# A hybrid decoder step: a lighter state-space mixer, with the sample states read out by C's high and low parts

## The chip, the cores and the metric

The kernel runs on one core of one Trainium2 chip. The metric is the device time of one execution in microseconds. A profiled execution gives a trace with the instructions of each engine: PE is TensorE (PEld its weight loads), DVE is VectorE, ACT is ScalarE, POOL is GpSimd, SP is SyncE, which here only issues DMAs. L333 means line 333 of the kernel before.

## The reference

One step of a one-layer hybrid decoder over 512 prompt tokens and 64 sample tokens (8 sequences of 8), width 2048. A combined projection of the normed input feeds a state-space branch (Mamba-2) and a sliding-window attention branch. Both are projected back, gated, added and projected once more. The part that the change touches, for one head, cut to its core:

```
Acs = cumsum(dt * A)                             # falls along a chunk
L[l, s] = exp(Acs[l] - Acs[s]) for s <= l, else 0
y_diag[l] = sum_s (C[l] . B[s]) L[l, s] X[s]
y_off[l]  = (C[l] . state_before) * exp(Acs[l])
state     = state * exp(Acs[last]) + sum_s exp(Acs[last] - Acs[s]) B[s] X[s]
g = (y_diag + y_off + d_skip * xs) * silu(z)
y = g * rsqrt(mean(g * g over the 512 of a group) + eps) * w
```

There are 64 heads of 64 in 8 groups; each group has its own B and C of 128 states. The prompt has four chunks of 128 tokens; each sample sequence is a chunk of 8 with a state of its own that is read, used and updated. Everything is float32, and all updated states are outputs.

## The kernel before

Activations lie with features on the partitions and all 576 tokens along the row. A projection takes a float32 weight apart into a high part `wh` (rounded to fp32r, a float format that PE takes in one pass) and a low part `wl` (the rest), and so the activations (`ah`, `al`); each product is three fp32r matmuls (L333). `run_main` goes over tiles of 128 output columns, 16 steps of six matmuls each, and calls `pump` after each step. A weight chunk is 1024 by 128, loaded by SP (L68) and split by ACT (L75) and DVE (L76), one chunk ahead. A finished tile stands in one of two PSUM buffers until its `take` has copied it out (for the convolved tiles `take_conv`, L809 to L811).

Everything else is written as generators: `pump` advances the first of the `quick` ones and, at rate 9 of 8, the first of the `jobs`. `yield` and `wait(n)` set after how many steps of the main stream a part is put. A planner of the framework then orders each engine's queue by its own estimate of when inputs are ready, with the order of writing as priority; on the chip each engine takes its queue in order. PSUM has besides a pool of four banks (`bank`), and each stage has pools of SBUF tiles (`kten` draws from N_K, `cten` from N_C); an instruction that needs a tile waits until one is free.

The stages: norm and first projections, 24 pairs of projection tiles by a seven-product scheme (L437), attention, then the state-space stage with its eight groups, then the three closing projections. In the state-space stage each group has six convolved tiles (B, C and four of x) and some gate tiles in the main stream, and one `ssd_job`, which starts when the group's last x tile is out, so beside the next group's projections:

- `lmat` builds the L matrix of four heads at a time: it loads the decay sums of the four heads, the same row to every partition (L859), subtracts each head's own sum per partition and takes the minimum with 0 on DVE (L862), and takes the exponential on ACT (L864). `mmat` multiplies with C.B (L870).
- Per chunk: transposes (L897), the old state by C (L912), the new state (L916), the diagonal part (`pairs_mm`, L848).
- `ssd_sample` does the eight sequences in two halves of four, each half in two pairs. It loads two states (L995), transposes each on PE (L1045), copies the transposed state `sT` out of PSUM on ACT (L1047), computes the addition to the state (L1054) and updates it (L1060), and reads out: a float32 matmul of C's eight columns, padded to 32 (`cpad`), by `sT` (L1066), into 32 partitions of a bank `pyo`. After each half the bank is copied (`yo`, L1073), turned back by four transposes (L1077) and multiplied into `ea` (L1080).
- The group's gated norm: squares and their sum on POOL (L957, L959), taken apart into two fp32r parts (L963, L964), summed over partitions by a matmul with ones so that every partition has the sum (L969); root (L970), reciprocal (L971), product (L975) and store to `y_d` (L977).

After the last group the attention output is loaded (L1242) and split (L1250, L1251) for the first closing projection.

Of the kernel before, what the change touches and what calls it, by code (L numbers as in the profile page):

```python
# [20 lines left out]
NB = 8  # L21
NQ = 8
NS = NB * NQ
T = NP_TOK + NS
TH = T // 2
DI = 4096
H = 64
G = 8
# [21 lines left out]
MIXES_S = (1, 1, 1, 1, 1, 1, 1, 1)  # L50
N_E = 14
N_C = 18
N_K = 18


def AP(t, off, dims):
    return bass.AP(t.tensor, t.offset + off, [list(d) for d in dims])
# [23 lines left out]
def hybrid(ctx, tc, x_prompt, x_sample, cache_k, cache_v, state_conv, state_ssm, norm_w, w_in, conv_w,  # L81
# [5 lines left out]
    ten, vec, act, pool, sync = nc.tensor, nc.vector, nc.scalar, nc.gpsimd, nc.sync  # L87
# [30 lines left out]
    xb_d = scratch([D // 2, TH], "xb_d")  # L118
    oh_d = scratch([HEADS * BL], "oh_d")
    ea_d = scratch([H, T], "ea_d")  # L120
    acs_d = scratch([H, T], "acs_d")
    e4_d = scratch([H, 4], "e4_d")
    e8_d = scratch([H, 8], "e8_d")

    def pers_tile(shape, name):
        return pers.tile(shape, F32, tag=name, name=name)

    ident = pers_tile([P, P], "ident")
    tri = pers_tile([P, P], "tri")
# [6 lines left out]
    sinks_s = pers_tile([P, 4], "sinks_s")  # L136
    dt_n = pers_tile([P, 5, H], "dt_n")
    dtd_n = pers_tile([P, 5, H], "dtd_n")
    acs_n = pers_tile([P, 5, H], "acs_n")
    cd_b = pers_tile([P, H, 4], "cd_b")  # L140
    dec_s = pers_tile([P, 32, 8], "dec_s")
    ones = pers.tile([P, P], F32R, tag="ones", name="ones")
# [129 lines left out]
    def kten(shape, name="k", dt=F32):  # L272
        return now["k"].tile(shape, dt, tag=now["kt"], name=name)
# [27 lines left out]
    def wait(n):  # L301
        for _ in range(n):
            yield
# [441 lines left out]
    def dt_job(dtT, bt):  # L745
# [14 lines left out]
        vec.scalar_tensor_tensor(out=x_, in0=x_, scalar=0.0, in1=p_, op0=ALU.max, op1=ALU.add)  # L760
        yield

        vec.tensor_scalar(out=s, in0=x_, scalar1=bt[:, 1:2], scalar2=-1.0, op0=ALU.mult, op1=ALU.mult)
        vec.tensor_tensor_scan(out=s2, data0=rst, data1=s, initial=0.0, op0=ALU.mult, op1=ALU.add)
        sync.dma_start(out=acs_d, in_=s2)
        act.activation(p_, s2, AF.Exp)
        sync.dma_start(out=ea_d, in_=p_)
        e4 = now["s"].tile([H, 4], F32, tag="e4", name="e4", bufs=1)
        e8 = now["s"].tile([H, 8], F32, tag="e8", name="e8", bufs=1)
# [5 lines left out]
        for lo, hi, n in ((0, 512, P), (512, T, 8)):  # L775
            v = s2[:, lo:hi].rearrange("p (c l) -> p c l", l=n)
            o = s[:, lo:hi].rearrange("p (c l) -> p c l", l=n)
            vec.tensor_tensor(out=o, in0=v[:, :, n - 1:n].to_broadcast([H, (hi - lo) // n, n]), in1=v,
                              op=ALU.subtract)
        act.activation(s, s, AF.Exp)  # L780
        vec.tensor_tensor(out=s, in0=s, in1=x_, op=ALU.mult)
        yield from wait(14)
        for srcT, dst in ((x_, dt_n), (s, dtd_n), (s2, acs_n)):
            ps = bank()
            for b in range(4):
                ten.transpose(ps[:, b * H:(b + 1) * H], srcT[:, b * P:(b + 1) * P], ident[:H, :H])
            ten.transpose(ps[:NS, 4 * H:5 * H], srcT[:, 512:T], ident[:H, :H])
            vec.tensor_copy(dst[:, 0:4, :], ps[:, 0:4 * H].rearrange("p (b h) -> p b h", h=H))
            vec.tensor_copy(dst[:NS, 4, :], ps[:NS, 4 * H:5 * H])
            yield  # L790
# [60 lines left out]
    def head_rows(t_, ea, g, c0, n):  # L851
        for hf in range(2):
            sync.dma_start(out=t_[64 * hf:64 * hf + 64], in_=AP(ea, (8 * g + hf) * T + c0, [[0, 64], [2 * T, 4], [1, n]]))

    def lmat(g, c0, n, blk, rows):
        out = []
        for q in range(2):
            l_ = kten([P, 4, P], "L")
            sync.dma_start(out=l_[:rows, :, :n], in_=AP(acs_d, (8 * g + 4 * q) * T + c0, [[0, rows], [T, 4], [1, n]]))  # L859
            for i in range(4):  # L860
                h = 8 * g + 4 * q + i
                vec.tensor_scalar(out=l_[:rows, i, :n], in0=l_[:rows, i, :n], scalar1=acs_n[:rows, blk, h:h + 1],  # L862
                                  scalar2=0.0, op0=ALU.subtract, op1=ALU.min)
            act.activation(l_[:rows, :, :n], l_[:rows, :, :n], AF.Exp)  # L864
            out.append(l_)
        return out

# [5 lines left out]
    def ssd_job(g):  # L873
# [89 lines left out]
        act.activation(th, tot, AF.Copy)  # L963
        pool.tensor_tensor(out=tl, in0=tot, in1=th, op=ALU.subtract)  # L964
        yield from wait(8)
        for s in range(2):
            ps = bank()
            for i, t_ in enumerate((th, tl)):
                ten.matmul(ps[:, :TH], ones, t_[:, s * TH:(s + 1) * TH], start=i == 0, stop=i == 1)  # L969
            act.activation(sqr[:, s * TH:(s + 1) * TH], ps[:, :TH], AF.Sqrt, bias=eps, scale=1.0 / 512)  # L970
        vec.reciprocal(sqr, sqr)  # L971
        yield
        for t in range(4):
            j = 4 * g + t
            vec.scalar_tensor_tensor(out=xs[t], in0=xs[t], scalar=prm[:, 240 + j:241 + j], in1=sqr, op0=ALU.mult,  # L975
# [11 lines left out]
    def ssd_sample(g, xs, bT, cT):  # L987
# [19 lines left out]
        for q in range(2):  # L1007
# [3 lines left out]
            pool.tensor_tensor(out=t_, in0=bq.unsqueeze(1).to_broadcast([P, 4, P]),  # L1011
                               in1=own.unsqueeze(2).to_broadcast([P, 4, P]), op=ALU.mult)
            bb.append(t_)
        cpad = kten([P, NB, 32], "cpad")
        pool.memset(cpad, 0.0)
        pool.tensor_copy(cpad[:, :, 0:8], cs_.rearrange("p (b q) -> p b q", q=8))
        yield
        px = bank()
        for t in range(4):
# [12 lines left out]
        yield from wait(2)  # L1032
        ea = kten([P, 4, NS], "eas")
        head_rows(ea, ea_d, g, 512, NS)
        for hb in range(2):
            pyo = bank()
            for b2 in range(2):
                sts, sTs = nxt, []
                b0 = 4 * hb + 2 * b2
# [2 lines left out]
                for i in range(2):  # L1042
                    ps = bank([P, 4, P])
                    for t in range(4):
                        ten.transpose(ps[:, t, :], sts[i][:, t, :], ident)  # L1045
                    sT = kten([P, 512], "sT")
                    act.activation(sT, ps.rearrange("p t n -> p (t n)"), AF.Copy)  # L1047
                    sTs.append(sT)
                    yield
                for u in range(2):  # L1050
                    ps = bank([P, 2, 2, P])
# [10 lines left out]
                                                     op0=ALU.mult, op1=ALU.add)  # L1062
                    yield
                for i in range(2):
                    bl = 2 * b2 + i
                    ten.matmul(pyo[32 * bl:32 * bl + 32, :], cpad[:, 4 * hb + bl, :], sTs[i], start=True, stop=True,  # L1066
                               tile_position=(0, 32 * bl))
                yield
                for i in range(2):
                    b = 4 * hb + 2 * b2 + i  # L1070
                    sync.dma_start(out=oview[b, 512 * g:512 * g + 512].rearrange("(t p) n -> p t n", p=P), in_=sts[i])
            yo = kten([P, 512], "yo")
            act.activation(yo, pyo, AF.Copy)  # L1073
            yield from wait(2)
            ps = bank([P, 4, P])
            for t in range(4):
                ten.transpose(ps[:, t, :], yo[:, t * P:(t + 1) * P], ident)  # L1077
            for t in range(4):
                v = ea[:, t, 32 * hb:32 * hb + 32].rearrange("p (b q) -> p b q", q=8)
                vec.tensor_tensor(out=v, in0=ps[:, t, :].rearrange("p (b q) -> p b q", q=32)[:, :, 0:8], in1=v,  # L1080
                                  op=ALU.mult)
            yield
        pd = bank([P, 4, P])
        pairs_mm(pd, xd[:NS], ls, NS)
        vec.tensor_tensor(out=ea, in0=pd[:, :, :NS], in1=ea, op=ALU.add)
# [363 lines left out]
```

## Time and profile before

| | us |
|---|---|
| median of 3 runs | 3288.77 (3287.61 to 3290.53) |
| profiled execution, its time | 3288.66 |
| profiled execution, span of the trace | 3286.6 |
| PE busy | 3191.1 |
| PE weight loads busy | 3025.2 |
| DVE busy | 1791.6 |
| ACT busy | 1336.9 |
| POOL busy | 332.1 |

Matmuls are pipelined, so the duration of one in the trace includes its way through the array; what a matmul costs in a full queue is the time from its start to the next one's start. A float32 matmul leaves two records, an fp32r matmul or a transpose one. A row of the timeline has start, length, engine, line, operation, output and inputs, shape and how many are merged; behind it in brackets idle time and what ended it. A row of the groups has busy time, mean ns of one, and the idle time ahead of them with its releasers. A row of the waits has the total, the number and the longest.

### The profile page before, as it was taken

How to read it: one execution, taken by the hardware profiler on the slowest of the kernel's cores; microseconds unless marked ns; L12 is line 12 of the kernel's file. 1: busy time of each engine (PE TensorE's matmuls, PEld its weight loads, DVE VectorE, ACT ScalarE, POOL GpSimd, SP SyncE). 2: the span in 40 equal slices, each digit the busy share in tenths (PEclk: the TensorE clock that was granted, in tenths of full speed). 3: DMA queues.
4: the chain of work that ended last, by engine and by line, in shares of the span. 5: the costliest groups of instructions: out<-in, count | busy, mean ns of one | idle time of the engine just before them, and what ended most of it. 6: DMA issues, size and time to landing. Idle time of an engine off the chain costs nothing. (4 is left out here: it accounts for less than half of the span.)

```text
span 3286.6 us, 57410 instructions
## 1 busy us (share of the span) xinstructions
PE 3191.1 (97%) x23323; PEld 3025.2 (92%) x23323; DVE 1791.6 (55%) x3290; ACT 1336.9 (41%) x2335; POOL 332.1 (10%) x443
## 2 busy tenths in 40 slices
PE   7989999999999999999999999999979999999997
PEld 6989999999988988989899898888869999999997
DVE  7666666622644444376786776766742242423554
ACT  5434444422445546345454445444531121211443
POOL 3200000000010110112212121121110000000111
PEclk9999999999999999999999999999989999999999
DMA  6564444433333243354554544645573353533555
GB/s 201 146 152 121 120 130 116 118 104 91 94 110 94 88 122 105 94 144 129 142 151 130 155 123 126 167 111 139 153 237 105 107 163 106 149 105 96 156 163 162
DMA packets 696823, 429.17 MB, mean 131 GB/s; under 512 B 39600, under 2 KB 661952, under 8 KB 696368
## 3 DMA queue, kind: packets, MB, share of 16 engines
q1 hardware_dynamic: 668000, 397.50, 43.5%
q10 hardware_dynamic: 15552, 15.93, 1.5%
q0 software_dynamic: 13008, 12.09, 1.4%
q8 instruction: 183, 3.00, 0.4%
q14 instruction: 80, 0.66, 0.1%
HBM read 361.00 MB, written 74.67 MB: 133 GB/s over the span
## 5 line engine op out<-in xcount | busy, mean ns | idle before, releaser
L333 PE MATMUL ps<-ah,wh 128*128 128x288 f32 (+2 forms) x5408 | 1235.7, 300 | 29.0 <-ACT craw L811 16.5
L333 PE MATMUL ps<-ah,wl 128*128 128x288 f32 (+2 forms) x5408 | 1231.9, 300 | 2.0 <-DVE wl L76 1.7
L333 PE MATMUL ps<-al,wh 128*128 128x288 f32 (+2 forms) x5408 | 1232.3, 299 | 0.0
L75 ACT ACTIVATE wh<-raw 128x1024 fp32r<-128x1024 f32 x538 | 570.0, 1060 | 1305.0 <-PE ps L333 866.4
L76 DVE TENSOR_TENSOR wl<-raw,wh 128x1024 fp32r<-128x1024 f32 x538 | 670.0, 1246 | 705.0 <-ACT wh L75 697.2
L333 PEld LDWEIGHTS ps<-ah,wh 128*128 128x128 f32 x5408 | 896.8, 191 | 54.5 <-issue 21.3
L333 PEld LDWEIGHTS ps<-ah,wl 128*128 128x128 f32 x5408 | 897.7, 191 | 28.4 <-issue 22.7
L333 PEld LDWEIGHTS ps<-al,wh 128*128 128x128 f32 x5408 | 898.3, 191 | 17.0 <-issue 14.5
L437 PE MATMUL ps<-ah,wh 128*128 128x288 f32 x768 | 227.7, 296 | 5.8 <-DVE w L391 5.8
L437 PE MATMUL ps<-ah,wl 128*128 128x288 f32 x768 | 228.0, 297 | 2.0 <-DVE wl L76 2.0
L437 PE MATMUL ps<-al,wh 128*128 128x288 f32 x768 | 227.6, 296 | 0.0
L827 DVE SCALAR_TENSOR_TENSOR cacc<-craw,prm,cacc 128x600 f32<-128x600 f32 x144 | 126.9, 890 | 52.0 <-ACT cacc L825 50.8
L437 PEld LDWEIGHTS ps<-ah,wh 128*128 128x128 f32 x768 | 145.4, 189 | 6.0 <-issue 6.0
L437 PEld LDWEIGHTS ps<-ah,wl 128*128 128x128 f32 x768 | 145.3, 189 | 2.5 <-DVE wl L76 2.5
L437 PEld LDWEIGHTS ps<-al,wh 128*128 128x128 f32 x768 | 145.4, 189 | 0.1
L377 DVE TENSOR_TENSOR raw<-raw 128x1024 f32<-128x1024 f32 x96 | 117.0, 1221 | 42.4 <-DMA raw<-in_w_in_dram 41.5
L1368 POOL TENSOR_TENSOR res<-res,fw 128x128 f32<-128x128 f32 (+3 forms) x35 | 31.8, 933 | 819.8 <-ACT junk L1364 787.5
L1060 DVE SCALAR_TENSOR_TENSOR s<-s,dec_s,bank 128x128 f32<-128x128 f32 x256 | 70.6, 341 | 61.0 <-PE bank L1054 61.0
L1314 DVE TENSOR_TENSOR sg<-ps,sg 128x576 f32<-128x576 f32 x32 | 24.2, 757 | 126.1 <-PE ps L333 126.1
L593 DVE CUSTOM_DVE_ANT_0 sc<-bank,bm 128x256 f32<-128x256 f32 (+1 forms) x128 | 43.8, 388 | 79.9 <-PE bank L589 71.1
L862 DVE TENSOR_SCALAR L<-L,acs_n 128x128 f32<-128x128 f32 (+1 forms) x320 | 75.0, 302 | 18.4 <-DMA L<-acs_d 18.1
L864 ACT ACTIVATE L<-L 128x512 f32<-128x512 f32 (+1 forms) x80 | 46.2, 585 | 63.7 <-DVE L L862 53.6
(503 smaller groups left out, 3617.3 us busy)
## 6 DMA issues: line engine op xcount, KB each, us to landing
raw<-in_w_in_dram SPq DMA_DIRECT2D x306, 512.0 KB
raw<-in_w_ssm_branch_dram SPq DMA_DIRECT2D x64, 512.0 KB
raw<-in_w_out_dram SPq DMA_DIRECT2D x64, 512.0 KB
L<-acs_d SPq DMA_DIRECT2D x64, 256.0 KB
s<-in_state_ssm_dram SPq DMA_DIRECT2D x64, 256.0 KB
out_dram<-s SPq DMA_DIRECT2D x64, 256.0 KB
raw<-in_w_attn_branch_dram SPq DMA_DIRECT2D x32, 512.0 KB
zs<-z_d SPq DMA_DIRECT2D x32, 288.0 KB
```

Of the source, the lines that this page charges most:

```text
L75: pin(nc.scalar.activation(wh, raw, AF.Copy))
L76: pin(nc.vector.tensor_tensor(out=wl, in0=raw, in1=wh, op=ALU.subtract))
L333: ten.matmul(sums[i][:, s, :part.shape[1]], a[:, kk, :], part, start=(k == 0 and q == 0), stop=(k == last and q == 2))
L377: vec.tensor_tensor(out=s_[x], in0=s_[a], in1=s_[b], op=op)
L437: ten.matmul(st[p]["ps", i][:, :TH], a[:, k, :], b, start=i < 4 and k == 0 and q == 0, stop=k == 7 and q == 2, skip_group_check=i >= 4)
L593: vec.tensor_tensor_reduce(out=s_[:, i, lo:256], in0=ps[:, i, lo:256], in1=bm[j][:, i, lo:256], scale=1.0, scalar=-3e38, op0=ALU.add, op1= ...
L827: vec.scalar_tensor_tensor(out=acc[:, :600], in0=raw[:, i:i + 600], scalar=prm[:, i * 48 + j:i * 48 + j + 1], in1=acc[:, :600], op0=ALU.mu ...
L862: vec.tensor_scalar(out=l_[:rows, i, :n], in0=l_[:rows, i, :n], scalar1=acs_n[:rows, blk, h:h + 1], scalar2=0.0, op0=ALU.subtract, op1=ALU ...
L864: act.activation(l_[:rows, :, :n], l_[:rows, :, :n], AF.Exp)
L1060: vec.scalar_tensor_tensor(out=sts[i][:, t, :], in0=sts[i][:, t, :], scalar=dec_s[:, 4 * g + t, b:b + 1], in1=ps[:, v, i, :], op0=ALU.mult ...
L1314: vec.tensor_tensor(out=sq(sg), in0=ps[:, :, :TH], in1=sq(sg), op=ALU.mult)
L1368: pool.tensor_tensor(out=res[b][:, qs], in0=res[b][:, qs], in1=fw[:rows, qs], op=ALU.mult)
```

## The change

In `lmat` the decay sums are kept with the other sign (`nacs`). One DVE operation takes the maximum with the partition's own sum for four heads together, and ACT takes four exponentials with scale -1 and the own sum as bias.

In the norm, one row of the sum over partitions is copied out (not the root on all 128), sent to DRAM (`rms_d`) and read back as 64 by 9; root and reciprocal are taken there, and the result goes to DRAM and comes back on all partitions. The four DMAs are issued by ACT, with `wait(6)` twice in between.

In `ssd_sample`, C's high part and low part stand side by side in one stationary tile of 128 columns per sequence (`cw_`, zero but for the eight columns of the sequence in each 64). The transposed state is taken apart as well (`sTh` by ACT, `sTl` by DVE), and two fp32r matmuls per sequence add into one bank for all eight sequences. That bank is copied once, and four float32 matmuls with `two` (two unit matrices of 64, one under the other) turn it back and add both halves. `N_K` goes from 18 to 19.

```diff
-N_K = 18
+N_K = 19
+    rms_d = scratch([G, 2, T], "rms_d")
+    two = pers_tile([P, 64], "two")
+    for hf in range(2):
+        pl = slice(64 * hf, 64 * hf + 64)
+        vec.tensor_copy(two[pl], ident[pl, pl])
...
-        vec.tensor_scalar(out=s, in0=x_, scalar1=bt[:, 1:2], scalar2=-1.0, op0=ALU.mult, op1=ALU.mult)
+        vec.tensor_scalar(out=s, in0=x_, scalar1=bt[:, 1:2], scalar2=None, op0=ALU.mult)
-        act.activation(p_, s2, AF.Exp)
+        act.activation(p_, s2, AF.Exp, scale=-1.0)
...
+            h = 8 * g + 4 * q
+            vec.tensor_tensor(out=l_[:rows, :, :n], in0=l_[:rows, :, :n],
+                              in1=nacs_n[:rows, blk, h:h + 4].unsqueeze(2).to_broadcast([rows, 4, n]), op=ALU.max)
             for i in range(4):
-                h = 8 * g + 4 * q + i
-                vec.tensor_scalar(out=l_[:rows, i, :n], in0=l_[:rows, i, :n], scalar1=acs_n[:rows, blk, h:h + 1],
-                                  scalar2=0.0, op0=ALU.subtract, op1=ALU.min)
-            act.activation(l_[:rows, :, :n], l_[:rows, :, :n], AF.Exp)
+                act.activation(l_[:rows, i, :n], l_[:rows, i, :n], AF.Exp, scale=-1.0,
+                               bias=nacs_n[:rows, blk, h + i:h + i + 1])
...
-            act.activation(sqr[:, s * TH:(s + 1) * TH], ps[:, :TH], AF.Sqrt, bias=eps, scale=1.0 / 512)
-        vec.reciprocal(sqr, sqr)
-        yield
+            act.activation(sqr[0:1, s * TH:(s + 1) * TH], ps[0:1, :TH], AF.Copy)
+        act.dma_start(out=rms_d[g, 0:1, :], in_=sqr[0:1, :])
+        rt = now["s"].tile([NS, 9], F32, tag="rt", name="rt", bufs=1)
+        act.dma_start(out=rt, in_=rms_d[g, 0].rearrange("(a b) -> a b", b=9))
+        yield from wait(6)
+        act.activation(rt, rt, AF.Sqrt, bias=eps[:NS], scale=1.0 / 512)
+        vec.reciprocal(rt, rt)
+        act.dma_start(out=rms_d[g, 1].rearrange("(a b) -> a b", b=9), in_=rt)
+        act.dma_start(out=sqr, in_=AP(rms_d[g, 1], 0, [[0, P], [1, T]]))
+        yield from wait(6)
...
-        cpad = kten([P, NB, 32], "cpad")
-        pool.memset(cpad, 0.0)
-        pool.tensor_copy(cpad[:, :, 0:8], cs_.rearrange("p (b q) -> p b q", q=8))
+        cw_ = [kten([P, 4, P], "cw", F32R) for _ in range(2)]
+        for q in range(2):
+            act.activation(cw_[q], ident.unsqueeze(1).to_broadcast([P, 4, P]), AF.Identity, scale=0.0)
+            c4 = cs_[:, 32 * q:32 * q + 32].rearrange("p (b q) -> p b q", q=8)
+            hi, lo = (AP(cw_[q], c0 + 32 * q, [list(cw_[q].ap[0]), [P + 8, 4], [1, 8]]) for c0 in (0, 64))
+            act.activation(hi, c4, AF.Copy)
+            vec.tensor_tensor(out=lo, in0=c4, in1=hi, op=ALU.subtract)
...
+        pyo = bank()
         for hb in range(2):
-            pyo = bank()
...
-                    sT = kten([P, 512], "sT")
-                    act.activation(sT, ps.rearrange("p t n -> p (t n)"), AF.Copy)
-                    sTs.append(sT)
+                    sTh, sTl = (kten([P, 4, P], n_, F32R) for n_ in ("sTh", "sTl"))
+                    act.activation(sTh, ps, AF.Copy)
+                    vec.tensor_tensor(out=sTl, in0=ps, in1=sTh, op=ALU.subtract)
+                    sTs.append((sTh, sTl))
...
-                    bl = 2 * b2 + i
-                    ten.matmul(pyo[32 * bl:32 * bl + 32, :], cpad[:, 4 * hb + bl, :], sTs[i], start=True, stop=True,
-                               tile_position=(0, 32 * bl))
+                    for d in range(2):
+                        ten.matmul(pyo, cw_[hb][:, 2 * b2 + i, :], sTs[i][d].rearrange("p t n -> p (t n)"),
+                                   start=b0 + i + d == 0, stop=b0 + i + d == 8, skip_group_check=True)
...
-            yo = kten([P, 512], "yo")
-            act.activation(yo, pyo, AF.Copy)
-            yield from wait(2)
-            ps = bank([P, 4, P])
-            for t in range(4):
-                ten.transpose(ps[:, t, :], yo[:, t * P:(t + 1) * P], ident)
-            for t in range(4):
-                v = ea[:, t, 32 * hb:32 * hb + 32].rearrange("p (b q) -> p b q", q=8)
-                vec.tensor_tensor(out=v, in0=ps[:, t, :].rearrange("p (b q) -> p b q", q=32)[:, :, 0:8], in1=v,
-                                  op=ALU.mult)
-            yield
+        yo = kten([P, 512], "yo")
+        act.activation(yo, pyo, AF.Copy)
+        yield from wait(2)
+        ps = bank([P, 4, NS])
+        for t in range(4):
+            ten.matmul(ps[:, t, :], yo[:, t * P:(t + 1) * P], two, start=True, stop=True)
+        vec.tensor_tensor(out=ea, in0=ps, in1=ea, op=ALU.mult)
+        yield
```

More of the change, by code (lines that the diff above doesn't have):

```diff
@@ L120, in hybrid @@
     ea_d = scratch([H, T], "ea_d")
-    acs_d = scratch([H, T], "acs_d")
+    nacs_d = scratch([H, T], "nacs_d")
     e4_d = scratch([H, 4], "e4_d")
     e8_d = scratch([H, 8], "e8_d")
+    rms_d = scratch([G, 2, T], "rms_d")
     def pers_tile(shape, name):
@@ L138, in hybrid @@
     dtd_n = pers_tile([P, 5, H], "dtd_n")
-    acs_n = pers_tile([P, 5, H], "acs_n")
+    nacs_n = pers_tile([P, 5, H], "nacs_n")
     cd_b = pers_tile([P, H, 4], "cd_b")
@@ L761, in dt_job @@
         yield
-        vec.tensor_scalar(out=s, in0=x_, scalar1=bt[:, 1:2], scalar2=-1.0, op0=ALU.mult, op1=ALU.mult)
+        vec.tensor_scalar(out=s, in0=x_, scalar1=bt[:, 1:2], scalar2=None, op0=ALU.mult)
         vec.tensor_tensor_scan(out=s2, data0=rst, data1=s, initial=0.0, op0=ALU.mult, op1=ALU.add)
-        sync.dma_start(out=acs_d, in_=s2)
-        act.activation(p_, s2, AF.Exp)
+        sync.dma_start(out=nacs_d, in_=s2)
+        act.activation(p_, s2, AF.Exp, scale=-1.0)
         sync.dma_start(out=ea_d, in_=p_)
@@ L777, in dt_job @@
             o = s[:, lo:hi].rearrange("p (c l) -> p c l", l=n)
-            vec.tensor_tensor(out=o, in0=v[:, :, n - 1:n].to_broadcast([H, (hi - lo) // n, n]), in1=v,
+            vec.tensor_tensor(out=o, in0=v, in1=v[:, :, n - 1:n].to_broadcast([H, (hi - lo) // n, n]),
                               op=ALU.subtract)
@@ L782, in dt_job @@
         yield from wait(14)
-        for srcT, dst in ((x_, dt_n), (s, dtd_n), (s2, acs_n)):
+        for srcT, dst in ((x_, dt_n), (s, dtd_n), (s2, nacs_n)):
             ps = bank()
@@ L858, in lmat @@
             l_ = kten([P, 4, P], "L")
-            sync.dma_start(out=l_[:rows, :, :n], in_=AP(acs_d, (8 * g + 4 * q) * T + c0, [[0, rows], [T, 4], [1, n]]))
+            sync.dma_start(out=l_[:rows, :, :n], in_=AP(nacs_d, (8 * g + 4 * q) * T + c0, [[0, rows], [T, 4], [1, n]]))
+            h = 8 * g + 4 * q
+            vec.tensor_tensor(out=l_[:rows, :, :n], in0=l_[:rows, :, :n],
+                              in1=nacs_n[:rows, blk, h:h + 4].unsqueeze(2).to_broadcast([rows, 4, n]), op=ALU.max)
             for i in range(4):
-                h = 8 * g + 4 * q + i
-                vec.tensor_scalar(out=l_[:rows, i, :n], in0=l_[:rows, i, :n], scalar1=acs_n[:rows, blk, h:h + 1],
-                                  scalar2=0.0, op0=ALU.subtract, op1=ALU.min)
-            act.activation(l_[:rows, :, :n], l_[:rows, :, :n], AF.Exp)
+                act.activation(l_[:rows, i, :n], l_[:rows, i, :n], AF.Exp, scale=-1.0,
+                               bias=nacs_n[:rows, blk, h + i:h + i + 1])
             out.append(l_)
```

## The prediction

> **What bounds the kernel now.** I read the busy shares first, then the state-space stage (the eight groups, 1344 to 2411 us) as one window, then TensorE's waits.
>
> ```profile
> PE 3191.1 (97%) x23323; PEld 3025.2 (92%) x23323; DVE 1791.6 (55%) x3290; ACT 1336.9 (41%) x2335; POOL 332.1 (10%) x443
> ...
> 1344.00:2411.00 1067.00, 1043.42 (x7602) 942.16 (x7600) 734.78 (x1478) 504.09 (x879) 193.82 (x260) 0.99 0.51 137
> ...
> PE ps L333 <- ACT craw L811: 16.5, 6, 4.6
> PE bank L969 <- ACT th L963: 13.0, 1, 13.0
> PE bank L1066 <- ACT sT L1047: 1.1, 2, 0.7
> ```
>
> The second row is the window: its length, then busy time on PE, PE's weight loads, DVE, ACT and POOL, granted clock, DMA share. PE is busy 1043 of 1067 us there; DVE is at 69%, ACT at 47%, DMA at 51%. PE's queue is in order, and in nearly every gap that the state-space work leaves, the projection matmuls of L333 stand ready. So a PE microsecond taken out of the stage is a microsecond of the kernel, as long as no new wait takes its place. The waits for the old read-out (L1066) are 1.1 us in all: its inputs are not late today. The two waits that matter are at the evictions of projection tiles (L811) and once behind the norm of the last group (L969).
>
> **Part 1, the read-out: C times the state, L1066.** It goes from 64 full-float matmuls with 32 stationary columns (two records each) to 128 one-record fp32r matmuls with 128 columns. I take prices as start-to-start, since ends are modelled.
>
> ```profile
> 1852.67 0.29 PE L333 MATMUL ps<-ah,wh 128*128 128x288 f32 x1
> 1852.90 1.05 PE L1066 MATMUL bank<-sT,cpad 128*32 128x512 f32 x2
> 1853.88 0.40 PE L333 MATMUL ps<-ah,wh 128*128 128x288 f32 x1
> 1854.11 0.42 PE L333 MATMUL ps<-al,wh 128*128 128x288 f32 x2
> 1854.46 1.04 PE L1066 MATMUL bank<-sT,cpad 128*32 128x512 f32 x2
> 1855.44 0.66 PE L1045 MATMUL bank<-ident,s 128*128 128x128 f32 x4
> ...
> 1942.18 0.39 PE L916 MATMUL bank<-xh,bh 128*128 128x512 f32 x1
> 1942.41 0.40 PE L916 MATMUL bank<-xh,bl 128*128 128x512 f32 x1
> 1942.64 0.30 PE L333 MATMUL ps<-al,wh 128*128 128x288 f32 x1
> 1942.78 0.42 PE L333 MATMUL ps<-ah,wl 128*128 128x288 f32 x2
> ...
> 1936.08 0.50 PE L916 MATMUL bank<-xl,bh 128*128 128x512 f32 x1
> 1936.51 0.65 PE L848 MATMUL bank<-L,xd 128*64 128x128 f32 x6
> ```
>
> One old read-out holds PE from 1852.90 to 1853.88, 0.98 us, and the same at 1854.46: 64 x 0.98 = 62.7 us. The L333 matmul just ahead of it takes 0.23 us where the one at 1942.64 takes 0.14, so entering the narrow shape costs about 0.09 more, up to 64 x 0.09 = 5.8 us that I keep as a bound. The new matmul has the form of L916 (fp32r, 128 by 128, 512 moving columns): 1942.18 to 1942.41 to 1942.64, 0.23 each, 128 x 0.23 = 29.4 us. In the dearest place a row shows, ahead of the 64-column shape, one takes 0.43; once for each of the 32 runs of four that is 6.4 us more. Gain 33.3 us, bounds 26.9 and 39.1. The accumulating bank is held over all four pairs of sequences, as two banks in turn are now, so three of four stay for the rest. The low parts need two more SBUF tiles a pair and the pool gains one: a state load may wait on SP until the pair before is read out, 4 x 0.23 = 0.9 us, with weight loads behind it that run ahead of their use, so nothing.
>
> **Part 2, the read-out turned back, L1077.** 64 transposes become 32 full-float matmuls against `two`, two records each, 64 columns wide.
>
> ```profile
> 2407.95 0.60 PE L1077 MATMUL bank<-ident,yo 128*128 128x128 f32 x4
> 2408.48 0.68 PE L848 MATMUL bank<-L,xd 64*64 64x64 f32 x16
> 2409.09 0.40 PE L333 MATMUL ps<-ah,wl 128*128 128x288 f32 x1
> ...
> 1809.85 1.05 PE L912 MATMUL bank<-xc,st 128*128 128x128 f32 x8
> 1810.66 0.50 PE L333 MATMUL ps<-al,wh 128*128 128x288 f32 x2
> ```
>
> Old: four in 0.53 us, 64 cost 8.5. New, 64 records: at most L912's 0.81 for 8 (twice as many moving columns), 6.5 us; at least L848's 0.61 for 16, 2.4 us. L912 has the same stationary shape, so I take it: gain 2.0, bounds 2.0 and 6.1. PE gains 35.3 us over the eight groups, 4.4 each.
>
> **Part 3, the other engines.** These run beside PE and I cost them at nothing on the path, with L333 as the cover.
>
> ```profile
> L862 DVE TENSOR_SCALAR L<-L,acs_n 128x128 f32<-128x128 f32 x256 | 61.2, 304 | 18.2 <-DMA L<-acs_d 18.1
> L870 DVE TENSOR_TENSOR L<-L,cb 128x512 f32<-128x512 f32 x64 | 42.1, 681 | 0.0
> L971 DVE RECIPROCAL sqr<-sqr 128x576 f32<-128x576 f32 x7 | 26.3, 3753 | 4.2 <-ACT sqr L970 4.2
> L864 ACT ACTIVATE L<-L 128x512 f32<-128x512 f32 x64 | 39.8, 629 | 60.9 <-DVE L L862 51.0 <-issue 6.2 <-POOL g L823 2.1
> L1047 ACT ACTIVATE sT<-bank 128x512 f32<-128x512 f32 x64 | 36.8, 596 | 67.9 <-PE bank L1045 46.7 <-issue 20.9
> L605 ACT ACTIVATE sc<-sc,nm 128x128 f32<-128x128 f32 x32 | 12.4, 389 | 3.4 <-DVE nm L600 3.4
> ```
>
> DVE per group: 32 wide L862 (9.7 us) become 8 whole-tile operations of L870's kind (5.4); the reciprocal of 3.75 shrinks to 9 elements a row; the new low parts of the states add 8 x 0.68 = 5.4. Net about -2.6. ACT per group: 8 exponentials of 0.63 (5.0) become 32 with a bias of their own, at most L605's 0.39 each (12.5); at least 0.63/4 each, no change. L605 is the nearer row: +7.5. Clearing and filling `cw` adds two of L1047's 0.60 and small copies; four DMA issues come on top. ACT goes from 47% to roughly 55%. The Trainium skill (ScalarE: Activation LUTs, What ACT_TABLE_LOAD costs) speaks against this split: it gives an activation with a pointer bias 280 ns plus 0.833 ns an element, less 93 ns of overlap back to back, so an estimate by that page is 0.29 us for each of the 32, 9.4 us a group. By it the sum on PE would be the same, as ACT stays far from full either way.
>
> The norm now goes through DRAM: four DMAs on ACT's queue, of which the second waits for the first to land and the fourth for the third. The nearest round trip is the L matrix: issued at 2009.32, used at 2011.59.
>
> ```profile
> 2009.32 0.68 SPq L859 DMA_DIRECT2D L<-acs_d  x1
> ...
> 2011.59 0.88 DVE L862 TENSOR_SCALAR L<-L,acs_n 128x128 f32<-128x128 f32 x4 [3.02 <-DMA L<-acs_d]
> ```
>
> At 2.3 us a trip, ACT can stand for 2 x 2.3 = 4.6 us a group. Behind it wait the weight split L75, the evictions L809 to L811 and, in the last group, the splits of the attention output L1250. Weight splits are made ahead of use and projection sums have two buffers, one full tile (96 x 0.14 = 13.4 us) ahead, so 4.6 hides; in the last group up to 4.6 us may show, bounds 0 and 4.6. I take 0, since only the projection after the attention one reads what the norm leaves. DMA volume hardly moves: 0.3 MB a group more. The sign change of the decay sums, `two` and the larger pool cost nothing on the path: DVE and SP are not last there.
>
> **The last group does not pay.** After its projections PE stands until the sums of squares are through POOL.
>
> ```profile
> 2410.64 0.43 PE L333 MATMUL ps<-ah,wl 128*128 128x288 f32 x2
> 2424.09 0.85 PE L969 MATMUL bank<-th,ones 128*128 128x288 f32 x2 [13.02 <-ACT th L963]
> ...
> 2411.29 4.06 POOL L957 TENSOR_TENSOR tot<-xc 128x576 f32<-128x576 f32 x1 [38.87 <-DVE xc L955]
> 2421.93 1.39 POOL L959 TENSOR_TENSOR tot<-tot,sqr 128x576 f32<-128x576 f32 x1
> ```
>
> The POOL chain is unchanged and starts where the sample work of that group ends; PE's 4.4 us there turn into a longer wait. So 7/8 of 35.3: **-30.9 us**, bounds 7/8 of 28.9 less 4.6, which is 20.7, and all of 45.2. From the profiled execution, 3288.66 us around its span of 3286.6, that is 3257.8; its 3288.66 stands within 0.1 us of the median 3288.77, so I predict **3258 us**, own range 3244 to 3268.
>
> **Rivals.**
>
> Groups' borders get better. At a border PE waits for a late eviction, then runs at half the clock:
>
> ```profile
> 2025.37 0.63 ACT L829 ACTIVATE xc<-cacc 128x512 f32<-128x512 f32 x1 [0.94 <-DVE cacc L827]
> 2026.86 0.85 PE L333 MATMUL ps<-ah,wh 128*128 128x288 f32 x2 [4.57 <-ACT craw L811]
> 2030.38 0.68 PE L333 MATMUL ps<-al,wh 128*128 128x288 f32 x2
> 2030.87 0.68 PE L333 MATMUL ps<-ah,wl 128*128 128x288 f32 x2
> ...
> 2025.30:2032.10 6.80, 5.24 (x22) 5.25 (x23) 0.79 (x2) 2.10 (x8) 6.49 (x11) 0.50 0.29 77
> ...
> 2059.56 0.53 PE L333 MATMUL ps<-ah,wh 128*128 128x288 f32 x2 [1.55 <-ACT craw L811]
> ```
>
> Two matmuls take 0.49 us there, 0.24 each against 0.14, so 22 of them lose 2.2 us. The six waits are two a border: three borders lose 6.6, with the 16.5 of waiting 23.1 us. ACT's SiLU waits for DVE there, and DVE gets 2.6 us lighter; if all borders clear, 3258 - 23 = 3235. Against: the lightening is small beside a 4.57 us wait. Chance 0.15.
>
> The read-out waits for DVE. The low part (0.68) stands behind ACT's high part and the state updates; if each of 32 runs waits for one, 21.8 us come back: 3280. For: a DVE step now lies between ACT's and the matmul, where there is none. Against: L333 stands between, and the stage leaves DVE 31% idle. Chance 0.15.
>
> Slower: late evictions at every border. ACT has more small work and stands for DMAs, so the eviction at L811 comes late in all eight groups, each 4.57 + 2.2 and the second wait of 1.55: 8 x 8.3 = 67, 44 above today's 23.1: 3258 + 44 = 3302. It decides from an ACT delay of more than the 13.4 us tile that the second buffer gives; today three of eight borders reach it. The Trainium skill (TensorE: Matmul & The Clock Gate, What's actually happening) would halve the clock only after an idle window of about 3.4 us; the trace agrees, 4.57 us of idling is followed by 0.50. Chance 0.12.
>
> It does not do what it says: the four-step norm and the split hold the jobs back so that the saved PE time is spent waiting in every group, 3285 to 3290. Against: 1.1 us of waits at L1066 now. Chance 0.08.
>
> **How the numbers follow.** Forecast 0.50 (3258), 0.15 (3235), 0.15 (3280), 0.12 (3302), 0.08 (about 3288). About 0.2%, 6.6 us, is what a measurement of this kernel can tell from no change. 3280 is 8.8 below the median, so about a fifth of that case, 0.03, falls into no change with most of the last, 0.06; of the last 0.01 each goes to faster and slower. Faster 0.50 + 0.15 + 0.12 + 0.01 = 0.78, same 0.09, slower 0.13. The range 3232 to 3284 holds the first three cases and leaves out the others.
>
> **What would show it.** Right: fp32r read-outs 0.23 us apart and nothing of the narrow shape; PE's busy time in the stage some 35 us less; groups some 4.4 us shorter; the wait at L969's successor as long or longer. Wrong: PE rows waiting for the low part of the states or for a bank; read-outs of two records; more waits for L811's successor with granted clock 0.50 after them; ACT standing at a DMA of rms_d with PE waiting behind it.

## The result and the profile after

The changed kernel takes 3236.53 us (3234.26 to 3236.98, 4 runs) beside 3288.19 us for the kernel before on the same chip: ratio 0.984, 95% interval 0.9823 to 0.9857, or 51.7 us less. That is inside the range on record (3232 to 3284), 21 us below the forecast of 3258 and 7 us below the prediction's own range for its sum (3244 to 3268). The profiled execution took 3234.26 us around a span of 3232.5; it is the fastest of the four, 2.3 us below their median. In the kernel after, the projection matmuls stand at L338, the evictions at L814 to L816, the read-out at L1087, the turning back at L1099.

From the page of the kernel after, the busy time of each engine:

```profile
PE 3145.6 (97%) x23323; PEld 3035.2 (94%) x23323; DVE 1782.0 (55%) x3076; ACT 1386.3 (43%) x2603; POOL 349.6 (11%) x427
```

The state-space stage between two fixed points of the main stream (the starts of the projection matmuls that follow the 8640th and the 14400th; L333 and L437 are counted, and they do the same in all kernels here), first before, then after; the columns are those of the prediction's window row:

```profile
1370.25:2472.36 1102.11, 1061.97 (x7701) 959.40 (x7699) 749.46 (x1489) 514.46 (x884) 204.68 (x261) 0.98 0.53 145
```

```profile
1371.70:2418.67 1046.97, 1016.34 (x7700) 968.32 (x7699) 739.28 (x1279) 563.96 (x1147) 220.99 (x245) 0.98 0.57 155
```

The stage is 55.1 us shorter, the whole span 54.1. PE's idle time in it went from 40.1 to 30.6 us, ACT is 49.5 us busier, DVE 10.2 less. PE's waits after, in total, number and longest:

```profile
PE ps L338 <- ACT craw L816: 9.6, 3, 3.2
PE ps L338 <- DVE mrg L1331: 8.5, 1, 8.5
PE bank L977 <- ACT th L970: 3.9, 2, 3.5
PE bank L1099 <- ACT yo L1095: 0.7, 1, 0.7
```

The evictions at the borders cost 9.6 us where they cost 16.5, the norm of the last group 3.9 where it cost 13.0, and a wait of 8.5 us at the first gate of the attention projection is new. Nothing waits for the low part of the states. At the end of the last group, POOL's sums of squares start at 2351.0, ahead of the last projection matmul (2359.78), where they started behind it before:

```profile
2351.00 2.93 POOL L964 TENSOR_TENSOR tot<-xc 128x576 f32<-128x576 f32 x1 [31.90 <-DVE xc L962]
...
2363.60 0.76 PE L977 MATMUL bank<-th,ones 128*128 128x288 f32 x2 [3.53 <-ACT th L970]
```

The new operations on PE's timeline after:

```profile
1959.79 0.29 PE L338 MATMUL ps<-al,wh 128*128 128x288 f32 x1
1959.92 0.39 PE L1087 MATMUL bank<-sTh,cw 128*128 128x512 f32 x1
1960.15 0.39 PE L1087 MATMUL bank<-sTl,cw 128*128 128x512 f32 x1
1960.38 0.29 PE L338 MATMUL ps<-al,wh 128*128 128x288 f32 x1
...
2346.80 1.10 PE L1099 MATMUL bank<-two,yo 128*128 128x64 f32 x8 [0.69 <-ACT yo L1095]
2347.83 0.68 PE L853 MATMUL bank<-L,xd 64*64 64x64 f32 x16
```

A read-out matmul is 0.23 us from start to start, as foreseen; the eight records of the turning back take 1.03 in this row (0.94 on the mean of all eight groups), not 0.81.

**A ledger of the stage.** From the starts of all PE matmuls between the two fixed points I took for each kernel: PE's idle time; the loss to the halved clock (half of the time of matmuls that started while the granted clock was 0.50); and the rest, PE's work at full clock. All sizes are in us. The time is the median; the other columns are from one profiled execution each, whose own time lies up to 3.8 us from that median (norm alone: 3254.6). "Evictions" is the wait for the last eviction of a projection tile (L811 before, L816 after) over the whole run.

| kernel | time | stage | work | idle | clock loss | evictions |
|---|---|---|---|---|---|---|
| before | 3288.2 | 1102.1 | 1044.9 | 40.1 | 17.1 | 16.5 |
| decay matrix alone | 3287.8 | 1102.4 | 1047.5 | 40.6 | 14.3 | 15.2 |
| read-out alone | 3269.5 | 1080.7 | 1006.4 | 57.2 | 17.2 | 38.7 |
| read-out and decay matrix | 3263.4 | 1075.7 | 1002.7 | 52.4 | 20.7 | 34.3 |
| norm alone | 3250.8 | 1064.7 | 1040.2 | 17.4 | 7.2 | 0 |
| read-out and norm | 3251.3 | 1060.4 | 1009.5 | 36.4 | 14.5 | 8.2 |
| all three (the change) | 3236.5 | 1047.0 | 1003.4 | 30.6 | 12.9 | 9.6 |

So of the 55.1 us, 41.5 are PE work, 9.5 idle time and 4.2 clock. Norm and decay matrix together without the read-out were not run.

### The profile page after: what moved, and what is told of

The parts are those of the page before. It is cut to its first block, busy times and chain, and to the rows that moved or that the text cites. A ratio compares the mean times of both kernels' runs of the same rounds, so it can differ in the third digit from the quotient of the medians.

```text
span 3232.5 us, 57506 instructions
## 1 busy us (share of the span) xinstructions
PE 3145.6 (97%) x23323; PEld 3035.2 (94%) x23323; DVE 1782.0 (55%) x3076; ACT 1386.3 (43%) x2603; POOL 349.6 (11%) x427
## 4 chain that ended last, share of the span: by engine, by line
PE 87%; DMA 6%; DVE 3%; ACT 2%; issue 1%; POOL 1%; SPq 0%; ACTq 0%; DVEq 0%; POOLq 0%
PE ps L338 60%; PE ps L442 16%; PE bank L637 1%; DMA raw<-in_w_out_dram 1%; PE bank L853 1%; PE bank L594 1%; DMA raw<-in_w_in_dram 1%; PE bank L1087 1%; PE bank L1065 1%; PE bank L627 1%; PE bank L923 1%; DVE wl L76 1%; PE bank L919 1%; ACT wh L75 1%; DMA L<-nacs_d 1%
## 5 line engine op out<-in xcount | busy, mean ns | idle before, releaser
L338 PE MATMUL ps<-ah,wh 128*128 128x288 f32 (+2 forms) x5408 | 1236.7, 300 | 25.4 <-ACT craw L816 9.6
L338 PE MATMUL ps<-ah,wl 128*128 128x288 f32 (+2 forms) x5408 | 1229.6, 299 | 2.0 <-DVE wl L76 1.8
L338 PE MATMUL ps<-al,wh 128*128 128x288 f32 (+2 forms) x5408 | 1229.9, 299 | 0.3 <-DVE al L1270 0.3
L338 PEld LDWEIGHTS ps<-ah,wh 128*128 128x128 f32 x5408 | 897.7, 191 | 39.3 <-issue 17.8
L338 PEld LDWEIGHTS ps<-ah,wl 128*128 128x128 f32 x5408 | 897.9, 190 | 17.5 <-issue 10.8
L338 PEld LDWEIGHTS ps<-al,wh 128*128 128x128 f32 x5408 | 897.8, 190 | 5.1 <-issue 2.4
L870 ACT ACTIVATE L<-L,nacs_n 128x128 f32<-128x128 f32 (+1 forms) x320 | 96.6, 379 | 61.0 <-DVE L L867 60.5
L867 DVE TENSOR_TENSOR L<-L,nacs_n 128x512 f32<-128x512 f32 (+1 forms) x80 | 54.0, 691 | 51.7 <-DMA L<-nacs_d 51.1
L911 POOL TENSOR_TENSOR xl<-xe,xh 128x512 fp32r<-128x512 f32 x32 | 56.7, 1772 | 201.1 <-ACT xh L910 182.0
```

The source lines that it names most:

```text
L338: ten.matmul(sums[i][:, s, :part.shape[1]], a[:, kk, :], part, start=(k == 0 and q == 0), stop=(k == last and q == 2))
L867: vec.tensor_tensor(out=l_[:rows, :, :n], in0=l_[:rows, :, :n], in1=nacs_n[:rows, blk, h:h + 4].unsqueeze(2).to_broadcast([rows, 4, n]), o ...
L870: act.activation(l_[:rows, i, :n], l_[:rows, i, :n], AF.Exp, scale=-1.0, bias=nacs_n[:rows, blk, h + i:h + i + 1])
L911: pool.tensor_tensor(out=xl, in0=xe, in1=xh, op=ALU.subtract)
```

## The experiments

Theory: the gain is PE's own time in the read-out, handed on one to one, with some waits moving. Rivals: the lighter mixer (decay matrix and norm) brings it; or the planner's new order does, whatever the work.

**The read-out alone.** The change without the edits of `lmat` and the norm; the sign of the decay sums as before.

```diff
-N_K = 18
+N_K = 19
...
+                    for d in range(2):
+                        ten.matmul(pyo, cw_[hb][:, 2 * b2 + i, :], sTs[i][d].rearrange("p t n -> p (t n)"),
+                                   start=b0 + i + d == 0, stop=b0 + i + d == 8, skip_group_check=True)
```

> The kernel before with the read-out alone (fp32r high and low parts, one bank, two unit matrices, pool of 19); decay matrix and norm as before. Theory (TensorE's work): 64 narrow float32 matmuls at 0.98 us plus the entry to and exit from the narrow shape become 128 at 0.23, some 35 us less TensorE work in eight groups, handed on one to one: about 3253 us, and the eviction waits at the borders of the groups may add or take 10. Rival 1 (the mixer brings it): at least half of the 52 us belongs to decay matrix and norm, so 3262 or more. Rival 2 (order): what counts is the planner's new order and not the work, so the time is not near 3253 in either direction and the TensorE busy time does not explain it.

Measured 3269.52 us, ratio 0.9942 (0.9927 to 0.9956): 20 us faster, not 35, and by its time rival 1's number. The ledger has both halves of the answer. PE's work is down by 38.5 us, as the theory wants. But idle time is up by 17.1: the waits at the evictions grow by 22.2 and that for the split of the attention output (L1258) by 5.7, while the wait behind the last group's norm falls by 9.1. The row of the stage, and two of the waits:

```profile
1370.18:2450.92 1080.74, 1023.58 (x7700) 971.59 (x7699) 781.42 (x1513) 521.89 (x906) 209.23 (x245) 0.97 0.54 148
...
PE ps L337 <- ACT craw L815: 38.7, 6, 9.7
PE bank L973 <- ACT th L967: 3.9, 1, 3.9
```

One of the six, at 2044 us, on three engines of this kernel's timeline (DVE, ACT, PE; L831 is the convolution, L833 its SiLU, L813 to L815 the evictions):

```profile
2038.34 3.75 DVE L975 RECIPROCAL sqr<-sqr 128x576 f32<-128x576 f32 x1 [0.48 <-ACT sqr L974]
2042.01 0.75 DVE L831 SCALAR_TENSOR_TENSOR cacc<-craw,prm,cacc 128x600 f32<-128x600 f32 x1
```

```profile
2042.79 0.63 ACT L833 ACTIVATE xc<-cacc 128x512 f32<-128x512 f32 x1 [1.30 <-DVE cacc L831]
2043.32 0.24 ACT L834 ACTIVATE xc<-cacc 128x64 f32<-128x64 f32 x1
2043.47 0.39 ACT L813 ACTIVATE craw<-ps 128x288 f32<-128x288 f32 x1
2043.76 0.35 ACT L814 ACTIVATE craw<-ps 128x224 f32<-128x224 f32 x1
2044.00 0.23 ACT L815 ACTIVATE craw<-ps 128x64 f32<-128x64 f32 x1
```

```profile
2044.28 0.85 PE L337 MATMUL ps<-ah,wh 128*128 128x288 f32 x2 [6.15 <-ACT craw L815]
2044.93 0.68 PE L337 MATMUL ps<-al,wh 128*128 128x288 f32 x2
```

Read downward: the norm's reciprocal holds DVE for 3.75 us; the last step of a convolution stands behind it; ACT's SiLU waits for that step; the eviction stands behind the SiLU; PE, 6.15 us idle, waits for the PSUM buffer and goes on at half the clock. So an instruction of the old norm that needs no PE at all takes back part of what the read-out gives. The same order, with ACT's SiLU waiting for a DVE step behind the reciprocal, stands at four of the six waits (1661, 1792, 2044 and 2175 us, 31.4 us together). At the two shorter ones (1917 and 2301 us, 3.64 each) the SiLU does not wait for DVE.

**The decay matrix alone.**

```diff
+            vec.tensor_tensor(out=l_[:rows, :, :n], in0=l_[:rows, :, :n],
+                              in1=nacs_n[:rows, blk, h:h + 4].unsqueeze(2).to_broadcast([rows, 4, n]), op=ALU.max)
             for i in range(4):
...
+                act.activation(l_[:rows, i, :n], l_[:rows, i, :n], AF.Exp, scale=-1.0,
+                               bias=nacs_n[:rows, blk, h + i:h + i + 1])
```

> The kernel before with the decay matrix alone (one maximum on VectorE for four heads, four exponentials with a bias on ScalarE). Theory: nothing of it is on TensorE's path: 3288 within 8 us, the rest being eviction waits that move. Rival 1: VectorE is 4 us a group lighter and the late evictions at three borders (23 us of waits and halved clock) clear: 3265 to 3275. Rival 2: any value up to 20 us away on either side, with the waits at the evictions changed.

Measured 3287.76 us, ratio 0.9995 (0.9986 to 1.0004): nothing. DVE's busy time in the stage falls by 26 us (749.46 to 723.10), ACT's rises by 45 (514.46 to 559.61), and the time shows neither:

```profile
1369.70:2472.10 1102.40, 1061.85 (x7700) 957.20 (x7700) 723.10 (x1255) 559.61 (x1116) 207.09 (x261) 0.98 0.53 145
```

**The norm alone.**

```diff
+            act.activation(sqr[0:1, s * TH:(s + 1) * TH], ps[0:1, :TH], AF.Copy)
+        act.dma_start(out=rms_d[g, 0:1, :], in_=sqr[0:1, :])
...
+        act.dma_start(out=sqr, in_=AP(rms_d[g, 1], 0, [[0, P], [1, T]]))
+        yield from wait(6)
```

> The kernel before with the norm alone (one row through DRAM, root and reciprocal on 64 by 9). Theory: off TensorE's path in seven groups; in the last group the four DMA trips come ahead of the first gates of the attention projection and cost 6 to 10 us, so 3288 to 3298. Rival 1: the reciprocal of 3.75 us on VectorE is gone, borders clear: 3265 to 3280.

Measured 3250.79 us, ratio 0.9882 (0.9865 to 0.9898): 38.7 us faster, three quarters of the whole change, with PE's work down by only 4.7. Theory and size are refuted, and rival 1 is outdone. The row of the stage, the waits and DVE at a border of this kernel:

```profile
1373.88:2438.59 1064.71, 1047.34 (x7700) 949.38 (x7699) 730.23 (x1489) 513.35 (x891) 213.12 (x261) 0.99 0.56 152
```

```profile
PE ps L334 <- ACT ah L1259: 5.1, 2, 4.2
PE bank L971 <- ACT th L964: 4.1, 1, 4.1
PE ps L334 <- DVE mrg L1321: 3.9, 1, 3.9
```

```profile
2028.52 0.84 DVE L828 SCALAR_TENSOR_TENSOR cacc<-craw,prm,cacc 128x600 f32<-128x600 f32 x1 [0.97 <-ACT cacc L826]
2030.07 0.21 DVE L978 RECIPROCAL rt<-rt 64x9 f32<-64x9 f32 x1 [0.70 <-ACT rt L977]
2030.20 1.65 DVE L828 SCALAR_TENSOR_TENSOR cacc<-craw,prm,cacc 128x600 f32<-128x600 f32 x2
```

No wait for an eviction is left. Idle time fell by 22.8 us (1102.11 - 1061.97 against 1064.71 - 1047.34) and the clock loss by 9.9.

**Read-out and decay matrix, without the norm.** The changed kernel with the lines of the norm as before.

```diff
-            act.activation(sqr[0:1, s * TH:(s + 1) * TH], ps[0:1, :TH], AF.Copy)
+            act.activation(sqr[:, s * TH:(s + 1) * TH], ps[:, :TH], AF.Sqrt, bias=eps, scale=1.0 / 512)
...
+        vec.reciprocal(sqr, sqr)
+        yield
```

> The changed kernel with the norm as before the change: read-out and decay matrix together. Theory: the wait of 8.5 us that the changed kernel has at the first gate of the attention projection, with the half clock after it, comes from the norm's DMA trips in the last group; without them 3236 less 6 to 9: 3227 to 3231, unless the borders of the groups get their waits back (up to 23 us: 3250). Rival 1: the norm carries part of the gain, 3245 or more, with more VectorE waits at the borders.

Measured 3263.43 us, ratio 0.9923 (0.9908 to 0.9938). Not 3227 and not even 3250: the eviction waits are back at 34.3 us, above the 16.5 of before. PE's work stays at 1002.7. Rival 1 holds.

**Read-out and norm, without the decay matrix.**

```diff
-            vec.tensor_tensor(out=l_[:rows, :, :n], in0=l_[:rows, :, :n],
-                              in1=nacs_n[:rows, blk, h:h + 4].unsqueeze(2).to_broadcast([rows, 4, n]), op=ALU.max)
             for i in range(4):
...
+                vec.tensor_scalar(out=l_[:rows, i, :n], in0=l_[:rows, i, :n], scalar1=acs_n[:rows, blk, h:h + 1],
+                                  scalar2=0.0, op0=ALU.subtract, op1=ALU.min)
```

> Read-out and norm together, the decay matrix as before the change. If the parts add: 3288 less 20 (read-out alone) less 39 (norm alone), 3230. If the eviction waits that the read-out alone has are what the norm clears, the read-out brings its whole TensorE time of about 38 here: 3251 less 38, 3213. If the decay matrix is needed for the gain: 3236 or more.

Measured 3251.31 us, ratio 0.9891 (0.9876 to 0.9905). Neither sum came out: the third case did. PE's work is down to 1009.5, 30.7 less than with the norm alone, but idle time and clock loss are 26.3 us more than there. The decay matrix is worth nothing alone and about 15 us on top of the two others; the ledger shows where (idle 36.4 to 30.6, work 1009.5 to 1003.4, clock 14.5 to 12.9), but no run shows which of its instructions does it.

**Each read-out matmul twice.** The state's part of the sample output is doubled; the sums, the banks and all else stay.

```diff
-                                   start=b0 + i + d == 0, stop=b0 + i + d == 8, skip_group_check=True)
+                                   start=b0 + i + d == 0, stop=False, skip_group_check=True)
+                        ten.matmul(pyo, cw_[hb][:, 2 * b2 + i, :], sTs[i][d].rearrange("p t n -> p (t n)"),
+                                   start=False, stop=b0 + i + d == 8, skip_group_check=True)
```

> The changed kernel with each of the 128 read-out matmuls issued twice into the same sum (the state's part of the sample output is doubled). Theory (TensorE's work is handed on one to one): 128 x 0.23 = 29.4 us more than the changed kernel in the seven groups and the last one, 3266 within 6. Rival (hidden or paced elsewhere): less than half of it, below 3251.

Measured 3265.79 us, ratio 0.9931 (0.9916 to 0.9946): 29.3 us above the changed kernel, against 29.4 expected. The stage has nearly the same idle time (1079.66 - 1048.69 = 31.0 against 30.6), though made up otherwise: no wait for an eviction is left, and other waits take its place.

```profile
1371.27:2450.93 1079.66, 1048.69 (x7828) 990.96 (x7827) 735.53 (x1279) 565.99 (x1149) 212.66 (x245) 0.99 0.56 150
```

```profile
1972.07 0.40 PE L1087 MATMUL bank<-sTh,cw 128*128 128x512 f32 x1
1972.31 0.39 PE L1089 MATMUL bank<-sTh,cw 128*128 128x512 f32 x1
1972.54 0.42 PE L338 MATMUL ps<-ah,wh 128*128 128x288 f32 x2
```

The agreement to 0.1 us is partly luck. The 128 added matmuls hold PE for 29.4 us (60.0 against 30.6 from start to next start), but PE's work rose by 34.3, as others became dearer, and the clock loss fell by 1.9; between the two profiled executions the span is 31.8 longer. Still, PE's time in the read-out is handed on, not hidden.

**What in the norm does it?** Three kernels from the one before. First the reciprocal over 9 of 576 columns:

```diff
-        vec.reciprocal(sqr, sqr)
+        vec.reciprocal(sqr[:, :9], sqr[:, :9])
```

> The kernel before with the reciprocal of the norm over 9 of 576 columns (the other columns stay unreciprocated, so the gated output is scaled wrongly; nothing else is left out). Theory A (VectorE's 3.75 us): the reciprocal stands in VectorE's queue between the convolution sums whose SiLU holds ScalarE's queue ahead of the evictions; without it the eviction waits go as they do with the norm alone, 3251 within 8. Theory B (spacing): the two waits of six steps put the norm elsewhere in the planner's order; then this stays at 3288 within 8.

Measured 3282.61 us, ratio 0.9988 (0.9978 to 0.9997): by its time theory B's number. The eviction waits and the wait of 13.0 us in the last group are gone, as theory A has it, but only some 5 us of time with them, for another wait stands in their place, for the decay matrix times C.B (L870) ahead of the diagonal part:

```profile
PE bank L848 <- DVE L L870: 24.1, 12, 3.9
```

Then the old norm with the change's spacing:

```diff
+        yield from wait(6)
         vec.reciprocal(sqr, sqr)
-        yield
+        yield from wait(6)
```

> The kernel before with the norm computed as before but spaced as in the change: six steps between root and reciprocal, six after it; no DRAM trip. Theory A (VectorE's 3.75 us): still there, 3280 to 3296. Theory B (spacing): 3251 within 8.

Measured 3288.1 us, ratio 0.9996 (0.9987 to 1.0006), with the eviction waits of before to the tenth (16.5 us, six, 4.6). Spacing alone does nothing. Last the norm through DRAM with the whole reciprocal behind the last trip:

```diff
-        vec.reciprocal(rt, rt)
...
         yield from wait(6)
+        vec.reciprocal(sqr, sqr)
```

> The norm alone with its DRAM trips, root on 64 by 9, but the reciprocal put back on VectorE over all 128 by 576 behind the last trip. Theory A: the 3.75 us of VectorE bring eviction waits back, 3270 to 3290. Theory B: 3251 within 8, as with the norm alone.

Measured 3270.16 us, ratio 0.9948 (0.9933 to 0.9963): half of the norm's gain is lost again, which is theory A's number, but not by its means. There is no eviction wait; idle time in the stage is 35.9 us with 24.0 of it from the last group's norm on (the longest waits there are 9.0, 7.7 and 6.6), where it was 17.4 with 12.8. So: with the whole reciprocal in its old place the eviction waits were 15 to 39 us in all five kernels; without it there they were 0 to 10.1 in all others. That the old reciprocal itself holds up the eviction is shown in the read-out alone, above. At the border of 2026 us in the kernel before it stood 18 us later, so there the mechanism is another. The border after that one, in the same kernel, shows it better:

```profile
2044.02 3.75 DVE L971 RECIPROCAL sqr<-sqr 128x576 f32<-128x576 f32 x1 [0.48 <-ACT sqr L970]
...
2155.85 1.06 ACT L75 ACTIVATE wh<-raw 128x1024 fp32r<-128x1024 f32 x1 [4.72 <-PE ps L333]
2156.93 1.28 ACT L829 ACT_TABLE_LOAD   x1
2158.22 0.63 ACT L829 ACTIVATE xc<-cacc 128x512 f32<-128x512 f32 x1
...
2159.43 0.23 ACT L811 ACTIVATE craw<-ps 128x64 f32<-128x64 f32 x1
2159.71 0.85 PE L333 MATMUL ps<-ah,wh 128*128 128x288 f32 x2 [3.63 <-ACT craw L811]
```

ACT's queue has a weight split, the load of SiLU's table (1.28 us) and the SiLU ahead of the eviction, and the split itself has waited 4.72 us for PE; so the eviction starts late and PE waits 3.63 us. How many of the 48 convolved tiles are evicted right behind a SiLU is a matter of the planned order: 12 in the kernel before, with the decay matrix alone and with the spacing; 19 in the two others with the old reciprocal; none with the norm alone or the short reciprocal, which have no eviction wait; 15 in the change. With the doubled read-out (9) and the reciprocal behind the trip (6) there are some, but no wait. So the norm's edit goes with another order of ACT's queue too; that this order alone makes the waits, and why the planner turns it, was not shown.

**The new wait at the first gate.** The changed kernel with the old norm in the last group alone.

```diff
+        if g == G - 1:
...
+                act.activation(sqr[:, s * TH:(s + 1) * TH], ps[:, :TH], AF.Sqrt, bias=eps, scale=1.0 / 512)
+            vec.reciprocal(sqr, sqr)
+            yield
+        else:
+            yield from row_norm(g, sqr, th, tl)
```

> The changed kernel with the norm of the last group alone as before the change (root and reciprocal on all 128 partitions, no DRAM). Theory: the wait of 8.5 us for the first gate of the attention projection and the halved clock behind it go, 6 to 8 us less than the changed kernel: 3228 to 3231; the seven groups ahead stay as they are. Rival: the gate's own load stands late on the DMA queue for another reason; the wait stays, 3236 within 3.

Measured 3234.28 us, ratio 0.9837 (0.982 to 0.9853): no difference from the change that can be told, and not the 3228 to 3231 of the theory. The wait at the gate (8.5 us) is gone, so it was the norm's, but the time is not; in its place PE waits for the split of the attention output:

```profile
PE ps L338 <- ACT craw L816: 10.0, 4, 3.2
PE ps L338 <- ACT ah L1281: 8.4, 2, 7.7
```

**The pool at 18.**

```diff
-N_K = 19
+N_K = 18
```

> The changed kernel with the tile pool at 18 as before. Theory (work): the one tile more only feeds the low parts; without it state loads wait on the DMA queue for the read-out of the pair before, TensorE does not: 3236 within 5. Rival (order): the pool moves the planner's order, and the time by more than 5 us.

Measured 3231.51 us, ratio 0.983 (0.9816 to 0.9845): the tile more is not needed for this time. **Both of the last two together:**

```diff
-N_K = 19
+N_K = 18
...
+        if g == G - 1:
...
+        else:
+            yield from row_norm(g, sqr, th, tl)
```

> The changed kernel with the pool at 18 and the norm of the last group as before the change. If the two small differences are real and add: 3236.5 less 5 less 2, 3229. If they are moves of the order within what any edit brings, 3229 to 3240, and TensorE's work in the stage stays at what the changed kernel has while its waits move.

Measured 3235.56 us, ratio 0.9832 (0.9817 to 0.9847). The small differences do not add; PE's work in the four kernels is 1003.4, 1003.7, 1004.0 and 1004.9 us. None of them is clear of the changed kernel.

## Why the prediction was right, and where it was not

The direction, the bound (PE) and the main means (the read-out's price) were right; the forecast gain was 21 us too small. By the ledger the stage gained 55.1 us where 30.9 were forecast. Of the 24 us between, 6.2 are PE work above the sum's 35.3, 4.4 are the eighth that the last group was not to pay, and 13.7 are idle time and clock, which stood at nothing. That the time still fell into the range on record owes something to luck: the read-out alone, for which the sum was made, gave 20 us, and without the norm's edit, costed at nothing, the change is 27 us slower.

- **What bounds the kernel.** Right. PE's work fell by 41.5 us and the stage by 55.1; doubling the read-out cost 29.3 of 29.4 us.
- **Part 1.** Right in mechanism, a little off in size. The new matmuls are 0.23 us apart; 128 of them take 30.6 us from start to next start in the stage, against 29.4. The old ones took 58.0, not 62.7: five pairs of the 64 ran side by side. So the read-out itself saves 27.3, not 33.3. The saving that I kept as a bound only is real and larger than the bound of 5.8: with the read-out alone PE's work fell by 38.5 us, so some 11 us come from the matmuls around it (projections 7.4, the addition to the state 3.0, transposes of the state 1.6). Only part of that is the entry into the narrow shape; the rest was not separated. That the sum lies near the upper bound of 39.1 is two errors that cancel.
- **Part 2.** 0.2 us gained, not 2.0: the new records took 7.5 us together, not 6.5 (0.94 for eight, more than L912's 0.81 for twice the columns, which I had taken as the upper end), and the old ones 7.7, not 8.5.
- **Part 3, "I cost them at nothing on the path".** This is the step that failed. It holds for the decay matrix alone (no change that can be told, with ACT 45 us busier in the stage); on top of the two others the decay matrix brings about 15 us. It fails most for the norm: alone it gains 38.7 us. I had named the reciprocal's 3.75 us, but added it to DVE's load per group, where 2.6 us look small beside 31% idle. What counted for the eviction waits was who waits behind it in DVE's queue, as four waits of the read-out alone show, and, as far as the kernels here go, in which order the evictions stand in ACT's queue. How the 38.7 us divide between these two and the end of the last group stays open: shortening the reciprocal in its place cleared the eviction waits and gained some 5 us only. ACT's exponentials were costed too high: one lasts 0.39 us, as L605's, but 248 of them in a row occupy ACT for 77 us, 0.31 each, 10.0 a group and not 12.5.
- **"The last group does not pay".** Failed too. The wait behind POOL's sums fell from 13.0 to 3.5 us. The sums take as long as before, but start at 2351.0, 9 us ahead of the last projection matmul of the group at 2359.8; before, POOL started at 2411.3, behind it (2410.6). Each of the read-out and the norm alone had the same effect (3.9 and 4.1 us); why the order turns so was not separated. What the norm's trips were to cost there, 0 to 4.6 us, was 8.5 at the gate, and taking them out only brought another wait of 7.7. All idle time of the stage from the last group's norm on went from 16.6 to 13.3 us, so the shorter wait was mostly spent again.
- **Rivals.** "Borders get better" came in part: 16.5 to 9.6 us. It hides two large moves against each other: the read-out alone makes them 38.7, the norm alone takes them away. That its 3235 is near the measured time is luck, since three waits of 3.2 us are left at the borders. The wait for DVE's low part did not come. Late evictions at every border did not come in the change; the read-out alone has six, four of them behind DVE's reciprocal, where the rival had ACT's small work and DMAs. The last rival, that the change does not do what it says, is out: PE's work fell and so did the time.

## What to carry to other kernels

When PE is the bound and other work fills its gaps, the PE time taken out is handed on, but the waits at the buffer hand-over can take half of it back, and clearing them can gain about as much. Price a long instruction of a side engine by what stands behind it in that queue at the hand-over, not by its share of the engine, and expect that shortening it can move the wait to another line. Parts of a change do not add: here they gave 0, 20 and 39 us alone, 26 and 36 in the two pairs that were run and 52 together, so a ledger of work, idle time and clock says more than a difference of times. Small edits that only moved the order could not be told apart here.

## What the hardware showed unexpectedly

The clock halved behind waits much shorter than the 4.57 us that the prediction shows (counted from the modelled end of the last matmul). In the kernel after, 6.8 us at 0.50 followed a wait of 3.22 us. In the kernel before, 3.41 us at 0.50 followed one of 2.59 us, and with the doubled read-out one of 1.89 us (up to 1946.44 us); the rows of the first two:

```profile
2143.03 0.85 PE L338 MATMUL ps<-ah,wh 128*128 128x288 f32 x2 [3.22 <-ACT craw L816]
...
2141.90:2148.70 6.80, 5.67 (x24) 5.60 (x25) 5.20 (x8) 6.13 (x14) 1.12 (x4) 0.50 0.43 106
```

```profile
1426.57 0.66 PE L848 MATMUL bank<-L,xd 128*64 128x128 f32 x8 [2.59 <-DVE L L870]
...
1427.96:1431.37 3.41, 3.41 (x17) 3.41 (x16) 3.41 (x6) 1.52 (x3) 0.00 (x0) 0.50 0.00 0
```

So the rule that the prediction cites for the halving, and its words that the trace agrees, do not cover these waits; behind the waits of 1.55 us in the kernel before the clock stayed full.

Going into a 32-column float32 matmul costs PE time that its own row does not show: ahead of the old read-out a projection matmul took 0.23 us from start to start (1852.67 to 1852.90), ahead of the new one 0.13 (1959.79 to 1959.92 above).
